# Row sums of reciprocals: the halves of a row paired, and one reciprocal for two elements

## The chip, the cores and the metric

The kernel runs on one core of a Trainium2 chip. The metric is the device time of one execution in microseconds (us); the times given are medians of several runs of the same program.

## The reference

```python
# x: (32, 512, 1024) float32, |N(0,1)| + 1e-6, all positive
def reference(x):
    return np.sum(1.0 / x, axis=-1).astype(np.float32)   # (32, 512)
```

There are 32 x 512 = 16384 rows of 1024 elements (67.1 MB), and each is reduced to one number, the sum of its reciprocals.

## The kernel before, in words

The 16384 rows are laid out as 128 partitions with 128 rows each; the view `x_v` (line 31) is `[p, f, d]`, so that one partition reads its rows from one contiguous stretch of memory. Each row is worked on whole, by one of two ways to a reciprocal, and then summed on VectorE. Nothing uses TensorE, and GpSimd (POOL) does nothing but set four constants.

The list `TILES` (line 23) cuts the 128 rows of a partition into groups `(ta, tv)`: 13 groups of (7, 1), smaller ones at the start and at the end. In a group:

- `tv` rows (17 in all) go to tile `xv` (line 66) by a DMA of their own (line 67), and VectorE takes their reciprocal in place (line 68).
- `ta` rows (111 in all) go to tile `xa` (line 69) by a second DMA (line 70). ScalarE makes the reciprocal of all of them with two passes over the flat tile, in place: Ln (line 72), then Exp with scale -1 (line 73), since exp(-ln x) = 1/x.
- Then VectorE sums every row of the group by `row_sum` (line 51; its instruction carries line 52): a custom operation that adds the first half of the row to the second, writes the 512 sums to `scratch`, and accumulates them into one column of `sums`. Each of these is followed on the engine by a short instruction that reads the accumulator out into that column.

At the end one DMA writes `sums` to the output (line 80). All DMAs are issued on SyncE's queue (SP), in the order of the loop. `apool` and `vpool` have five buffers each, and a load is issued only once its buffer has been freed by the last row sum that reads it. The order of the instructions on each engine isn't written out by hand: the framework's scheduler sets it when the kernel is built and may move an instruction past others of its engine; at run time every engine goes through its own in that fixed order and waits for what each needs.

Of the kernel before, what the change touches and what calls it, by code (L numbers as in the profile page):

```python
# [1 line left out]

# [5 lines left out]


@with_exitstack
def kernel(
    ctx: ExitStack,
    tc: tile.TileContext,
    x: bass.AP,
    out: bass.AP,
):
    nc = tc.nc
    P = 128
    D = 1024  # L20
    F = 128

    TILES = [(2, 0), (3, 1), (6, 1)] + [(7, 1)] * 13 + [(4, 1), (3, 1), (2, 0)]
    assert sum(a + v for a, v in TILES) == F
    assert sum(v for a, v in TILES) == 17

    Ln = mybir.ActivationFunctionType.Ln
    Exp = mybir.ActivationFunctionType.Exp
    HALF = slice(None, D // 2), slice(D // 2, None)

    x_v = x.flatten_outer_dims().rearrange("(p f) d -> p f d", p=P)
    out_v = out.flatten().rearrange("(p f) -> p f", p=P)

    act_sets = list(get_activation_tables(nc.m.arch).keys())
    nc.scalar.add_instruction(  # L35
        mybir.InstLoadActFuncSet(
            name=nc.get_next_instruction_name(),
            act_func_set_id=act_sets.index("natural_log_exp_and_others"),
            ins=[],
            outs=[],  # L40
        )
    )

    apool = ctx.enter_context(tc.tile_pool(name="apool", bufs=5))
    vpool = ctx.enter_context(tc.tile_pool(name="vpool", bufs=5))
    opool = ctx.enter_context(tc.tile_pool(name="opool", bufs=1))

    sums = opool.tile([P, F], mybir.dt.float32)
    scratch = opool.tile([P, D // 2], mybir.dt.float32)

    def row_sum(src, c):
        nc.vector.tensor_tensor_reduce(  # L52
            out=scratch,
            in0=src[:, HALF[0]],
            in1=src[:, HALF[1]],
            scale=1.0,
            scalar=0.0,
            op0=mybir.AluOpType.add,
            op1=mybir.AluOpType.add,
            accum_out=sums[:, c : c + 1],  # L60
        )

    c0 = 0
    for t, (ta, tv) in enumerate(TILES):
        if tv:
            xv = vpool.tile([P, tv, D], mybir.dt.float32, tag="xv")
            nc.sync.dma_start(out=xv, in_=x_v[:, c0 + ta : c0 + ta + tv, :])
            nc.vector.reciprocal(out=xv, in_=xv)  # L68
        xa = apool.tile([P, ta, D], mybir.dt.float32, tag="xa")
        nc.sync.dma_start(out=xa, in_=x_v[:, c0 : c0 + ta, :])  # L70
        flat = xa.rearrange("p t d -> p (t d)")
        nc.scalar.activation(out=flat, in_=flat, func=Ln)  # L72
        nc.scalar.activation(out=flat, in_=flat, func=Exp, scale=-1.0)  # L73
        for j in range(ta):
            row_sum(xa[:, j], c0 + j)
        for j in range(tv):
            row_sum(xv[:, j], c0 + ta + j)
        c0 += ta + tv

    nc.sync.dma_start(out=out_v, in_=sums)  # L80


# [1 line left out]
_INS = ['x']  # L84
_OUTS = [((32, 512), 'float32')]


# [23 lines left out]
```

## Time and profile before

| | |
|---|---|
| median of 3 runs | 214.5 us (214.32 to 214.5) |
| span of the profiled execution, first to last instruction | 212.4 us |
| median less span: what lies around the span | 2.1 us |
| VectorE (DVE) busy | 197.0 us, 93% of the span |
| ScalarE (ACT) busy | 196.5 us, 92% |
| GpSimd (POOL) busy | 0.2 us |
| read from HBM | 67.11 MB, mean 316 GB/s over the span |

The profile is of one execution, and its time beyond the span isn't given apart from the runs'; the 2.1 us are the median of the runs less that span. Busy time counts an engine's instructions that compute; the share of 16 DMA engines can read a little over 1 in a short window, where packets overlap. A line such as L72 is line 72 of the kernel.

### The profile page before, as it was taken

Reading aid. Unit: us, or ns where it says so; the run is one execution under the profiler, and the core shown is the slowest. Engines: PE = TensorE matmul, PEld = TensorE weight load, DVE = VectorE, ACT = ScalarE, POOL = GpSimd, SP = SyncE. Lnnn points to the kernel's source line nnn. Section 1 sums busy time; section 2 is a strip of 40 time slices with the busy share of each in tenths; the row PEclk is TensorE's granted clock in tenths of the full one; section 3 lists DMA queues with packets and bytes.
Section 4 is the critical chain, followed back from the end, with each engine's and each line's share of the span. In section 5 each row is a group of like instructions: output and inputs, shape, how many; then the busy total and the mean of one; then the engine's idle time right before and its main releaser. Section 6 shows DMA issues by size and latency. Waiting matters only on the chain. (4 is left out here: it accounts for less than half of the span.)

```text
span 212.4 us, 455 instructions
## 1 busy us (share of the span) xinstructions
DVE 197.0 (93%) x273; ACT 196.5 (92%) x39; POOL 0.2 (0%) x4
## 2 busy tenths in 40 slices
DVE  0799999999999999999999999999999999999994
ACT  2794999999999999999999999999999999999960
POOL 0000000000000000000000000000000000000000
DMA  6999999999999999999998987969590715000000
GB/s 241 424 470 420 432 444 432 417 390 464 402 433 443 433 444 432 412 432 417 408 441 351 444 346 304 432 239 428 200 435 37 316 79 197 0 0 0 0 0 12
DMA packets 5330, 67.19 MB, mean 316 GB/s; under 512 B 592, under 2 KB 720, under 8 KB 2896
## 3 DMA queue, kind: packets, MB, share of 16 engines
q1 hardware_dynamic: 5328, 67.18, 75.4%
q14 instruction: 2, 0.02, 0.0%
HBM read 67.11 MB, written 0.07 MB: 316 GB/s over the span
## 5 line engine op out<-in xcount | busy, mean ns | idle before, releaser
L68 DVE RECIPROCAL xv<-xv 128x1024 f32<-128x1024 f32 x17 | 111.3, 6547 | 6.8 <-DMA xv<-in_x_dram 6.8
L72 ACT ACTIVATE xa<-xa 128x7168 f32<-128x7168 f32 (+4 forms) x19 | 98.2, 5174 | 7.7 <-DMA xa<-in_x_dram 7.7
L73 ACT ACTIVATE xa<-xa 128x7168 f32<-128x7168 f32 (+4 forms) x19 | 98.5, 5187 | 0.5
L52 DVE CUSTOM_DVE_ANT_0 scratch<-xa 128x512 f32<-128x512 f32 x111 | 75.8, 682 | 5.4 <-ACT xa L73 2.1
L52 DVE CUSTOM_DVE_ANT_0 scratch<-xv 128x512 f32<-128x512 f32 x17 | 11.7, 688 | 0.6
L52 DVE DVE_READ_ACCUMULATOR2_ANT sums<- 128x1 f32 x128 | 10.5, 82 | 0.0
L35 ACT ACT_TABLE_LOAD x1 | 1.3, 1283 | 0.7 <-PEq L95 0.7
L95 POOL MEMSET const-bfloat16-1.0<- 128x1 bf16 x1 | 0.1, 101 | 0.0
L95 POOL MEMSET const-uint8-127<- 128x1 uint8 x1 | 0.1, 101 | 0.0
L95 POOL MEMSET const-float32-0.0<- 128x1 f32 x1 | 0.1, 98 | 0.2 <-issue 0.2
L95 POOL MEMSET const-float32-1.0<- 128x1 f32 x1 | 0.1, 98 | 0.0
## 6 DMA issues: line engine op xcount, KB each, us to landing
xa<-in_x_dram SPq DMA_DIRECT2D x13, 3584.0 KB, 21.3
xv<-in_x_dram SPq DMA_DIRECT2D x17, 512.0 KB, 9.7
xa<-in_x_dram SPq DMA_DIRECT2D x2, 1536.0 KB, 7.8
xa<-in_x_dram SPq DMA_DIRECT2D x1, 3072.0 KB, 16.3
xa<-in_x_dram SPq DMA_DIRECT2D x2, 1024.0 KB, 4.8
xa<-in_x_dram SPq DMA_DIRECT2D x1, 2048.0 KB, 7.9
out_dram<-sums SPq DMA_DIRECT2D x1, 64.0 KB, 1.6
```

The costliest lines, as they stand in the source:

```text
L35: nc.scalar.add_instruction(mybir.InstLoadActFuncSet(name=nc.get_next_instruction_name(), act_func_set_id=act_sets.index("natural_log_exp_ ...
L52: nc.vector.tensor_tensor_reduce(out=scratch, in0=src[:, HALF[0]], in1=src[:, HALF[1]], scale=1.0, scalar=0.0, op0=mybir.AluOpType.add, op ...
L68: nc.vector.reciprocal(out=xv, in_=xv)
L72: nc.scalar.activation(out=flat, in_=flat, func=Ln)
L73: nc.scalar.activation(out=flat, in_=flat, func=Exp, scale=-1.0)
L95: nc = _bacc.Bacc("TRN2", target_bir_lowering=False, num_devices=1)
```

## The change

The reciprocals of two elements are taken from one reciprocal of their product: 1/a + 1/b = (a + b)/(ab). A row's first half is a, its second half b.

- The 128 rows of a partition are cut into 19 groups (`GROUPS`): (2,0), (3,1), fourteen of (7,1), (4,1), (2,1), (1,1). A group is one tile `xt` and one DMA (110 rows are paired, 18 are whole). There are four `xt` buffers.
- Paired rows are worked on in chunks of up to four (33 chunks in all, 28 of them in the groups of (7,1): one of four rows, one of three). GpSimd multiplies the halves into tile `pr`. ScalarE takes Ln of `pr` in place, with a scale S = 2^17, then Exp with scale -1 into tile `rc`, which lies in PSUM (two buffers of four banks). VectorE then does for each row one multiply and sum over 1024 elements: the row, seen as 2 x 512, times `rc` broadcast twice, times S, written over the row and accumulated into a column of `sums`.
- A whole row is done by ScalarE alone: Ln in place, then Exp in place with the accumulator output into its column of `sums`.
- VectorE's reciprocal, the tile `scratch` and the separate loads of `xv` are gone.

```diff
-    TILES = [(2, 0), (3, 1), (6, 1)] + [(7, 1)] * 13 + [(4, 1), (3, 1), (2, 0)]
+    GROUPS = [(2, 0), (3, 1)] + [(7, 1)] * 14 + [(4, 1), (2, 1), (1, 1)]
+    CH = 4
+    S = float(2**17)
...
-    apool = ctx.enter_context(tc.tile_pool(name="apool", bufs=5))
-    vpool = ctx.enter_context(tc.tile_pool(name="vpool", bufs=5))
+    xpool = ctx.enter_context(tc.tile_pool(name="xpool", bufs=4))
+    ppool = ctx.enter_context(tc.tile_pool(name="ppool", bufs=4))
     opool = ctx.enter_context(tc.tile_pool(name="opool", bufs=1))
+    rpool = ctx.enter_context(
+        tc.tile_pool(name="rpool", bufs=2, space=bass.MemoryType.PSUM)
+    )
...
-    for t, (ta, tv) in enumerate(TILES):
-        if tv:
-            xv = vpool.tile([P, tv, D], mybir.dt.float32, tag="xv")
-            nc.sync.dma_start(out=xv, in_=x_v[:, c0 + ta : c0 + ta + tv, :])
-            nc.vector.reciprocal(out=xv, in_=xv)
-        xa = apool.tile([P, ta, D], mybir.dt.float32, tag="xa")
-        nc.sync.dma_start(out=xa, in_=x_v[:, c0 : c0 + ta, :])
-        flat = xa.rearrange("p t d -> p (t d)")
-        nc.scalar.activation(out=flat, in_=flat, func=Ln)
-        nc.scalar.activation(out=flat, in_=flat, func=Exp, scale=-1.0)
-        for j in range(ta):
-            row_sum(xa[:, j], c0 + j)
-        for j in range(tv):
-            row_sum(xv[:, j], c0 + ta + j)
-        c0 += ta + tv
+    for np_, ns in GROUPS:
+        n = np_ + ns
+        xt = xpool.tile([P, n, D], f32, tag="xt")
+        nc.sync.dma_start(out=xt, in_=x_v[:, c0 : c0 + n, :])
+        for s in range(0, np_, CH):
+            m = min(CH, np_ - s)
+            pr = ppool.tile([P, m, H], f32, tag="pr")
+            nc.gpsimd.tensor_tensor(
+                out=pr, in0=xt[:, s : s + m, :H], in1=xt[:, s : s + m, H:], op=mult
+            )
+            nc.scalar.activation(out=pr, in_=pr, func=Ln, scale=S)
+            rc = rpool.tile([P, m, H], f32, tag="rc")
+            nc.scalar.activation(out=rc, in_=pr, func=Exp, scale=-1.0)
+            for j in range(m):
+                row = xt[:, s + j, :].rearrange("p (h e) -> p h e", h=2)
+                nc.vector.tensor_tensor_reduce(
+                    out=row,
+                    in0=row,
+                    in1=rc[:, j, :].unsqueeze(1).to_broadcast([P, 2, H]),
+                    scale=S,
+                    scalar=0.0,
+                    op0=mult,
+                    op1=add,
+                    accum_out=sums[:, c0 + s + j : c0 + s + j + 1],
+                )
+        if ns:
+            nc.scalar.activation(out=xt[:, np_:n, :], in_=xt[:, np_:n, :], func=Ln)
+            for j in range(np_, n):
+                nc.scalar.activation(
+                    out=xt[:, j, :],
+                    in_=xt[:, j, :],
+                    func=Exp,
+                    scale=-1.0,
+                    accum_out=sums[:, c0 + j : c0 + j + 1],
+                )
+        c0 += n
```

## Rows read from the trace of the kernel before

**Rows 1.** The page: busy time, and the span in 40 slices.

```profile
DVE 197.0 (93%) x273; ACT 196.5 (92%) x39; POOL 0.2 (0%) x4
...
DMA  6999999999999999999998987969590715000000
```

**Rows 2.** Timeline, one period: start us, us, engine, line, tiles, shapes, idle before.

```profile
54.24 6.16 ACT L72 ACTIVATE xa<-xa 128x7168 f32<-128x7168 f32 x1
...
54.37 0.69 DVE L52 CUSTOM_DVE_ANT_0 scratch<-xa 128x512 f32<-128x512 f32 x1 [0.15 <-ACT xa L73]
...
55.10 0.69 DVE L52 CUSTOM_DVE_ANT_0 scratch<-xa 128x512 f32<-128x512 f32 x1
...
56.45 6.55 DVE L68 RECIPROCAL xv<-xv 128x1024 f32<-128x1024 f32 x1
60.44 6.18 ACT L73 ACTIVATE xa<-xa 128x7168 f32<-128x7168 f32 x1
...
66.52 6.16 ACT L72 ACTIVATE xa<-xa 128x7168 f32<-128x7168 f32 x1
```

**Rows 3.** SP's waits: who waited for whom, us in total, times, longest us.

```profile
SPq L67 <- DVE sums L52: 133.6, 12, 16.8
```

**Rows 4.** Windows by stage: engines' busy us, clock, DMA share, GB/s.

```profile
0.00:2.00 2.00, 0.00 (x0) 1.27 (x1) 0.20 (x4) 1.00 0.19 41
2.00:5.60 3.60, 0.00 (x0) 0.01 (x1) 0.00 (x0) 1.00 0.94 366
5.60:24.00 18.40, 16.94 (x15) 14.23 (x5) 0.00 (x0) 1.00 1.03 440
24.00:60.00 36.00, 34.99 (x40) 35.91 (x7) 0.00 (x0) 1.00 1.01 429
60.00:118.00 58.00, 56.20 (x86) 57.84 (x11) 0.00 (x0) 1.00 0.98 417
118.00:185.00 67.00, 65.20 (x86) 66.81 (x12) 0.00 (x0) 1.00 0.66 269
```

**Rows 5.** Groups of instructions, shapes apart: busy us, mean ns, idle before.

```profile
L68 DVE RECIPROCAL xv<-xv 128x1024 f32<-128x1024 f32 x17 | 111.3, 6547 | 6.8 <-DMA xv<-in_x_dram 6.8
...
L72 ACT ACTIVATE xa<-xa 128x7168 f32<-128x7168 f32 x13 | 80.1, 6160 | 0.0
L52 DVE CUSTOM_DVE_ANT_0 scratch<-xa 128x512 f32<-128x512 f32 x111 | 75.8, 682 | 5.4 <-ACT xa L73 2.1
L52 DVE CUSTOM_DVE_ANT_0 scratch<-xv 128x512 f32<-128x512 f32 x17 | 11.7, 688 | 0.6
L52 DVE DVE_READ_ACCUMULATOR2_ANT sums<- 128x1 f32 x128 | 10.5, 82 | 0.0
...
L72 ACT ACTIVATE xa<-xa 128x3072 f32<-128x3072 f32 x2 | 5.5, 2754 | 1.0 <-DMA xa<-in_x_dram 1.0
```

**Rows 6.** DMA issues of the page: count, KB each, us to landing.

```profile
xa<-in_x_dram SPq DMA_DIRECT2D x13, 3584.0 KB, 21.3
xv<-in_x_dram SPq DMA_DIRECT2D x17, 512.0 KB, 9.7
```

**Rows 7.** Timeline, the end: the last row sum and the output's DMA.

```profile
209.16 0.69 DVE L52 CUSTOM_DVE_ANT_0 scratch<-xa 128x512 f32<-128x512 f32 x1
209.78 0.08 DVE L52 DVE_READ_ACCUMULATOR2_ANT sums<- 128x1 f32 x1
209.89 0.34 SPq L80 DMA_DIRECT2D out_dram<-sums  x1
```

More of the change, by code (lines that the diff above doesn't have):

```diff
@@ L18 @@
     nc = tc.nc
+    f32 = mybir.dt.float32
     P = 128
     D = 1024
+    H = D // 2
     F = 128
-    TILES = [(2, 0), (3, 1), (6, 1)] + [(7, 1)] * 13 + [(4, 1), (3, 1), (2, 0)]
-    assert sum(a + v for a, v in TILES) == F
-    assert sum(v for a, v in TILES) == 17
+    CH = 4
+    S = float(2**17)
+    GROUPS = [(2, 0), (3, 1)] + [(7, 1)] * 14 + [(4, 1), (2, 1), (1, 1)]
+    assert sum(a + b for a, b in GROUPS) <= F
     Ln = mybir.ActivationFunctionType.Ln
     Exp = mybir.ActivationFunctionType.Exp
-    HALF = slice(None, D // 2), slice(D // 2, None)
+    mult = mybir.AluOpType.mult
+    add = mybir.AluOpType.add
     x_v = x.flatten_outer_dims().rearrange("(p f) d -> p f d", p=P)
@@ L42 @@
     )
-    apool = ctx.enter_context(tc.tile_pool(name="apool", bufs=5))
-    vpool = ctx.enter_context(tc.tile_pool(name="vpool", bufs=5))
+    xpool = ctx.enter_context(tc.tile_pool(name="xpool", bufs=4))
+    ppool = ctx.enter_context(tc.tile_pool(name="ppool", bufs=4))
     opool = ctx.enter_context(tc.tile_pool(name="opool", bufs=1))
[L48 to L61, printed above, removed]
@@ new lines @@
+    sums = opool.tile([P, F], f32)
+    c0 = 0
+    for np_, ns in GROUPS:
[34 more added lines that the diff above has]
+        c0 += n
@@ L80 @@
+    assert c0 == F, c0
     nc.sync.dma_start(out=out_v, in_=sums)
```

## The prediction

> **What bounds the kernel now.** I read the page first, then one period of the timeline, SP's waits and the windows by stage. The page shows VectorE and ScalarE both busy over 92% of the span, while the DMA line runs full for its first half and then thins out [rows 1]. In the timeline one group of eight rows takes 66.52 - 54.24 = 12.28 us on ScalarE, whose two passes follow each other without a gap, and VectorE waits 0.15 us a period for ScalarE [rows 2]. So both engines set the pace, at 12.28 us for eight rows (4.19 MB, 342 GB/s). The loads aren't the limit: SP stands 133.6 us waiting for row sums to free buffers [rows 3]. Left alone, the DMA runs faster: 440, 429 and 417 GB/s in three stretches at a share of 0.98 to 1.03, and 269 GB/s once the buffers are full [rows 4]. The question is how far the engines fall below the loads' own pace of 8 x 0.5243 MB / 429 GB/s = 9.78 us for eight rows, and what follows the last load.
>
> **ScalarE.** It now passes over half-length products of 110 rows and whole rows of 18. From the forms of 7168 and 3072 elements [rows 5]: (6160 - 2754) / 4096 = 0.8315 ns an element, and 2754 - 3072 x 0.8315 = 200 ns fixed. A pair of passes starts 12.28 us after the one before although it lasts 6.16 + 6.18 us [rows 2], so 0.06 is taken off a pair. A (7,1) group has 2 x (2048 + 1536 + 1024) = 9216 elements in six instructions: 7.66 + 1.20 - 0.18 = 8.68 us. The accumulator's read-out on ScalarE is in no row; VectorE's takes 82 ns [rows 5], so I add 0.08 (bounds 0 and 0.20, a whole fixed part): 8.76 us. Exp into PSUM isn't shown either: anything from a gain to a loss of one fixed part, 0.20 for each of two Exps; I take none, since the same stream with 0.4 more, 9.2, stays below 9.78. In all: 149504 elements x 0.8315 = 124 us, 102 instructions x 0.20 = 20, less 51 x 0.06, plus 1: 143 us where it was 196.5.
>
> **VectorE.** The 17 reciprocals go (111.3 us), and 128 sums over 512 pairs become 110 over 1024. A 512-element sum takes 0.69 us, and the next one starts 0.73 after it [rows 2, 5]. How the new one grows is in no row. At least by 512 elements at ScalarE's rate: 0.69 + 0.43 = 1.12. At most by a second 512 less the fixed part, which can't be much below the 0.08 of the one-element read-out: 0.69 + 0.61 = 1.30. I take the middle, 1.21, and 0.04 to the next start: 1.25 us a row, 8.75 us a group (8.1 to 9.4), 137 us in all. The operand in PSUM is unshown; the nearest rows are these two-input float32 sums, so I add nothing, and as the upper end 0.20 (a rival below).
>
> **GpSimd.** Its only rows here are constants, 0.2 us in all [rows 1]. A product of 512 pairs is nearest to VectorE's two-input 512-element sum, 0.69 us; the far end is half a reciprocal of 1024, 3.27 us [rows 5]. I take 0.69: 2.8 us for four rows, 4.8 us a group, 76 in all. It decides nothing until 9.78 / 7 = 1.40 us a row.
>
> The Trainium skill, "GPSIMD Engine Reference", section "Performance versus the Vector engine", speaks against this placing: an elementwise float32 operation of two inputs over 2048 elements is given 4497 ns there, about twice VectorE's time. By that estimate a chunk of four rows takes 4.5 us and a group 7.9, still under 9.78, and the sum below would be 178.1; no run here shows it.
>
> **Loads and waits.** Eight rows now come by one DMA instead of two. One of 3.5 MB takes 21.3 us from issue to landing, behind others in the queue [rows 6], so size isn't new; issues fall from 37 to 20 and stay hidden behind transfers. Five buffers of each kind become four. A buffer is held for its load (9.8), the first product (2.8), Ln and Exp of 2048 (3.7), seven rows on VectorE (8.75), and some 2.5 of issue and start: 27.6 us, against 4 x 9.78 = 39.1 at the loads' pace. So 11 us are spare and SP always has a further load queued. New are ScalarE's waits for GpSimd, with Exp and the whole row queued behind, and VectorE's for Exp; in the steady state each engine idles about 1 us a group, and nobody downstream is late, because the next data lands only after 9.78 us.
>
> **The sum.** The loads bound all but the ends. By 5.6 us, 2.0 x 41 + 3.6 x 366 GB/s = 1.40 MB have come [rows 4]; the other 65.71 MB at 429 take 153.2 us: last landing 158.8. (At 440, 154.9; at 417, 163.2.) The last (7,1) group lands ten rows, 12.2 us, earlier. ScalarE starts it 2.8 us later and ends it 8.8 after that, 0.6 before the last landing. Then, by the same prices, (4,1) takes 5.9, (2,1) 4.2 and (1,1) 3.3 us, all landed and multiplied by then: 12.7 after the last landing, 13.0 with two hand-offs of 0.15 [rows 2]. VectorE's last row ends before that, at 11.9. From the last sum, at 209.86, to the end of the span it took 2.5 us [rows 7]. Span: 158.8 + 13.0 + 2.5 = 174.3 us, against 212.4. Around the profiled span 2.1 us lie to the median of 214.5: **176.4 us**.
>
> **Rivals.**
>
> *ScalarE or VectorE still sets the pace.* If the PSUM operand costs VectorE 0.20 a row, a group takes 7 x 1.45 = 10.15 us; over fourteen groups that is 5 us more, about 182. It decides from 1.40 us a row. The same price comes from an order in which ScalarE stands before a whole row whose load is still under way: the scheduler does move work forward, as the reciprocal at 56.45 among older sums shows [rows 2]. One group too early fits into the 11 us spare; two hold a buffer for some 41 us, 0.4 a group over 39.1: again 182.
>
> *The read rate doesn't hold.* Rates fall from stretch to stretch [rows 4]; 417 throughout gives 163.2 + 15.5 + 2.1 = 181. At 342 GB/s, the pace of the kernel before, it would be 5.6 + 192.1 + 15.5 + 2.1 = 215, no gain at all; a fall far below 417 gets 0.01.
>
> A rule of the Trainium skill goes that way: "SBUF — State Buffer", section "Summary: rules for kernel authors", tells one to reckon transfers between HBM and SBUF at about 358 GB/s, and by that this kernel would take 207 us. The trace speaks against it: 429 GB/s over 36 us.
>
> *GpSimd is slow.* At x us a row the time is 5.6 (first landing) + 110 x + 3 (last passes) + 4.6 (the end): 13.2 + 110 x. It passes the loads from x = 1.48, is 214.5 at x = 1.83 and 373 at the far end.
>
> *GpSimd and VectorE shut each other out (slower).* Both work in SBUF at the same time, which nothing in this trace shows, since GpSimd did nothing [rows 1]. If a product can't run while a row sum does, the two add up: 0.69 + 1.25 = 1.94 a row, 13.2 + 110 x 1.94 = 227 us. It decides from a sum of 1.83. For it speaks that GpSimd has been left free of such work so far and no row excludes it; against it, that the new sum reads only one operand from SBUF.
>
> The Trainium skill bears on that: "SBUF — State Buffer", section "Who interferes with whom", has VectorE keep GpSimd's reads out only with two inputs in SBUF or in a two-port mode, and here the reciprocals are in PSUM; no run here shows it.
>
> *The change doesn't run as overlapped as written.* VectorE writes its products back over the tile whose later rows GpSimd still has to read. If the second product waited for the first four rows, a group would be a chain: 2.8 + 3.7 + 5.0 + 2.1 = 13.6 us, fourteen of them 190, with 19 before and 23 after: 232 us.
>
> **How the numbers follow.** Loads as the bound, 172 to 181 by their rate: 0.67, since three engines each come in under 9.78 us at their own rows' prices. ScalarE, VectorE or the order sets the pace (181 to 190): 0.14. GpSimd between 1.48 and 1.83: 0.04, beyond it 0.03. Loads far slower, but short of 215: 0.01. Shut out 0.07, chained 0.03, no visible change 0.01. Faster is 0.67 + 0.01 + 0.14 + 0.04 = 0.86, slower 0.13; the bound of 0.2%, 0.4 us, is about what a measurement of this kernel can tell from no change. The range is 171 to 195: below, 440 GB/s (-3.9) and a gain on PSUM; above, the engines' rivals and GpSimd up to 1.65. It leaves out some 0.16.
>
> **What would show it.** Right: a DMA line at 9 until about 159 us, a read-out's DMA some 15 us later; ScalarE and VectorE at about 140 us of busy time, idling before products and Exp. Wrong: gaps in the DMA line before 150 us; a product over 1.4 us a row, or longer when a row sum runs beside it; row sums over 1.4 us; VectorE or ScalarE without idle time in the middle.

## The result, and the profile after

The changed kernel takes 180.19 us (four runs, 180.13 to 180.47) against 214.44 for the kernel before, measured again beside it: a ratio of 0.8406, 95% interval 0.8394 to 0.8417. Forecast were 176.4 us, faster, and a range of 171 to 195. The span of the profiled execution is 178.0 us, with 2.1 to 2.2 around it as before; the sum had 174.3.

From the page of the changed kernel, engines and the DMA line, to be laid beside [rows 1]:

```profile
DVE 127.0 (71%) x220; ACT 141.5 (79%) x121; POOL 125.2 (70%) x37
DMA  6999999999998999999999999999999999851000
```

VectorE and ScalarE were at 93 and 92% and are now at 71 and 79%. No engine is the bound by its share; the DMA line is the one that stays at 9, for 32 of 40 slices. The windows by stage say it in GB/s (columns as in [rows 4]):

```profile
5.60:24.00 18.40, 5.88 (x10) 9.43 (x10) 9.59 (x3) 1.00 1.00 430
24.00:60.00 36.00, 24.23 (x42) 30.24 (x24) 28.80 (x9) 1.00 1.01 437
60.00:118.00 58.00, 48.47 (x84) 50.57 (x43) 46.80 (x13) 1.00 1.01 433
118.00:185.00 67.00, 48.39 (x84) 49.95 (x45) 39.72 (x11) 1.00 0.60 253
```

The groups of instructions with shapes apart (columns as in [rows 5]) have the new prices:

```profile
L81 DVE CUSTOM_DVE_ANT_1 xt<-xt,rc 128x1024 f32<-128x1024 f32 x110 | 126.9, 1217 | 48.5 <-issue 38.3 <-ACT rc L78 10.2
L73 POOL TENSOR_TENSOR pr<-xt 128x2048 f32<-128x2048 f32 x15 | 67.9, 4528 | 31.0 <-DMA xt<-in_x_dram 31.0
L73 POOL TENSOR_TENSOR pr<-xt 128x1536 f32<-128x1536 f32 x15 | 51.8, 3452 | 2.5 <-DMA xt<-in_x_dram 2.5
L76 ACT ACTIVATE pr<-pr 128x2048 f32<-128x2048 f32 x15 | 28.5, 1897 | 3.0 <-POOL pr L73 2.9
L78 ACT ACTIVATE rc<-pr 128x2048 f32<-128x2048 f32 x15 | 28.0, 1864 | 0.0
...
L94 ACT ACTIVATION_READ_ACCUMULATOR xt<-xt 128x1 f32 x18 | 3.4, 186 | 0.0
```

A row sum over 1024 elements costs 1217 ns, a product of four rows 4528 ns, and GpSimd's idle time stands in front of the first product of a group, until a load lands. Who waits for whom, in us, times, and the longest:

```profile
POOL pr L73 <- DMA xt<-in_x_dram: 38.6, 16, 6.3
ACT pr L76 <- POOL pr L73: 27.0, 18, 5.9
```

The first engine of the chain waits for data, the second for the first. SP waits for freed buffers about as long as before [rows 3], 147.7 us in 15 waits, but now other loads are under way meanwhile: the DMA share stays at 1.00 to 1.01 until 118 us. GpSimd's timeline shows the pace (two products of a group in one line, x2), and where it ends:

```profile
88.78 7.95 POOL L73 TENSOR_TENSOR pr<-xt 128x2048 f32<-128x2048 f32 x2 [1.77 <-DMA xt<-in_x_dram]
98.49 7.94 POOL L73 TENSOR_TENSOR pr<-xt 128x2048 f32<-128x2048 f32 x2 [1.77 <-DMA xt<-in_x_dram]
...
148.03 15.98 POOL L73 TENSOR_TENSOR pr<-xt 128x2048 f32<-128x2048 f32 x5 [2.75 <-DMA xt<-in_x_dram]
```

98.49 - 88.78 = 9.71 us a group, and every group begins when a load lands. The last (7,1) group landed at 148.03. From there the end is told by ScalarE's and VectorE's timelines:

```profile
152.59 1.91 ACT L76 ACTIVATE pr<-pr 128x2048 f32<-128x2048 f32 x1 [0.50 <-POOL pr L73]
156.01 1.48 ACT L76 ACTIVATE pr<-pr 128x1536 f32<-128x1536 f32 x1 [1.50 <-POOL pr L73]
157.40 3.23 ACT L78 ACTIVATE rc<-pr 128x2048 f32<-128x2048 f32 x2
...
159.38 1.22 DVE L81 CUSTOM_DVE_ANT_1 xt<-xt,rc 128x1024 f32<-128x1024 f32 x1 [2.62 <-issue]
...
174.23 1.22 DVE L81 CUSTOM_DVE_ANT_1 xt<-xt,rc 128x1024 f32<-128x1024 f32 x1
...
175.48 0.35 SPq L104 DMA_DIRECT2D out_dram<-sums  x1
```

The instruction at 156.01 is the second chunk's Ln. It stands on ScalarE in front of the first chunk's Exp (157.40), although the program text has them the other way, and it waits 1.50 us for the second product. So VectorE, which had nothing to do for 2.62 us (the profile names no releaser there; Exp's end is the one that fits), gets its first reciprocals at 159.3. Then it sums 14 rows without a gap, 1.142 us apart, to 175.4.

### The profile page after: what moved, and what is told of

It is laid out like the page before. It is cut to its first block, busy times and chain, and to the rows that moved or that the text cites. A ratio compares the mean times of both kernels' runs of the same rounds, so it can differ in the third digit from the quotient of the medians.

```text
span 178.0 us, 550 instructions
## 1 busy us (share of the span) xinstructions
DVE 127.0 (71%) x220; ACT 141.5 (79%) x121; POOL 125.2 (70%) x37
## 5 line engine op out<-in xcount | busy, mean ns | idle before, releaser
L81 DVE CUSTOM_DVE_ANT_1 xt<-xt,rc 128x1024 f32<-128x1024 f32 x110 | 126.9, 1217 | 48.5 <-issue 38.3
L73 POOL TENSOR_TENSOR pr<-xt 128x1536 f32<-128x1536 f32 (+3 forms) x33 | 125.0, 3808 | 38.6 <-DMA xt<-in_x_dram 38.6
L76 ACT ACTIVATE pr<-pr 128x1536 f32<-128x1536 f32 (+3 forms) x33 | 53.4, 1618 | 27.1 <-POOL pr L73 27.0
L78 ACT ACTIVATE rc<-pr 128x1536 f32<-128x1536 f32 (+3 forms) x33 | 51.2, 1579 | 0.1
L92 ACT ACTIVATE xt<-xt 128x1024 f32<-128x1024 f32 x18 | 18.8, 1042 | 3.6 <-DMA xt<-in_x_dram 3.6
L94 ACT ACTIVATE xt<-xt 128x1024 f32<-128x1024 f32 x18 | 19.0, 1056 | 0.5
L81 DVE DVE_READ_ACCUMULATOR2_ANT sums<- 128x1 f32 x110 | 9.1, 83 | 0.0
L94 ACT ACTIVATION_READ_ACCUMULATOR xt<-xt 128x1 f32 x18 | 3.4, 186 | 0.0
```

The lines of the kernel that those rows point to most:

```text
L73: nc.gpsimd.tensor_tensor(out=pr, in0=xt[:, s : s + m, :H], in1=xt[:, s : s + m, H:], op=mult)
L76: nc.scalar.activation(out=pr, in_=pr, func=Ln, scale=S)
L78: nc.scalar.activation(out=rc, in_=pr, func=Exp, scale=-1.0)
L81: nc.vector.tensor_tensor_reduce(out=row, in0=row, in1=rc[:, j, :].unsqueeze(1).to_broadcast([P, 2, H]), scale=S, scalar=0.0, op0=mult, op ...
L92: nc.scalar.activation(out=xt[:, np_:n, :], in_=xt[:, np_:n, :], func=Ln)
L94: nc.scalar.activation(out=xt[:, j, :], in_=xt[:, j, :], func=Exp, scale=-1.0, accum_out=sums[:, c0 + j : c0 + j + 1],)
```

## The experiments

The first four ask what the loads, the order, PSUM and the number of buffers are worth.

**e1: ScalarE in the order of the program text.**

Every pass of ScalarE goes through `act`, which adds an edge of order, without a wait, behind the pass before it.

```diff
+    def act(**kw):
+        i = nc.scalar.activation(**kw)
+        i = getattr(i, "ins", i)
+        if last[0] is not None:
+            tc.add_manual_dep(
...
+        last[0] = i
...
-            nc.scalar.activation(out=pr, in_=pr, func=Ln, scale=S)
+            act(out=pr, in_=pr, func=Ln, scale=S)
```

> ScalarE's instructions are kept in the order of the program text, so that each Exp stands right behind its Ln; nothing else changes. Theory (the order on ScalarE is part of the last stretch): Exp of the last (7,1) group's first chunk no longer waits for the second product, so it starts some 2.9 us earlier, the 1.5 us gap on ScalarE there closes, and the end moves by about 2.0 us: 178.2 us, with the steady period unchanged at 9.71 us. Rival (the loads bound everything, an order on an engine with spare time costs nothing): 180.2 us.

179.69 us, 0.5 less: the expectation was 1.5 too hopeful. ScalarE's end in e1's timeline:

```profile
154.85 1.88 ACT L68 ACTIVATE rc<-pr 128x2048 f32<-128x2048 f32 x1
...
172.36 0.60 ACT L68 ACTIVATE rc<-pr 128x512 f32<-128x512 f32 x1
172.89 2.13 ACT L68 ACTIVATE xt<-xt 128x1024 f32<-128x1024 f32 x2
```

Exp does start at 154.85 instead of 157.40. But now ScalarE ends last: the text's order leaves a whole row (2.13 us and its read-out) behind the last Exp, where the scheduler had put it in front. It is also dearer throughout: a group, gap taken off, takes 8.87 us (83.97 to 93.70 less 0.86), where the changed kernel's order takes 8.59 (84.02 to 93.73 less 1.12). Another order does it in 8.33 (e3b).

**e2: the reciprocals in SBUF.**

```diff
-        tc.tile_pool(name="rpool", bufs=2, space=bass.MemoryType.PSUM)
+        tc.tile_pool(name="rpool", bufs=2)
```

> The tile rc lies in SBUF instead of PSUM, so that VectorE's row sum reads two inputs from SBUF while GpSimd multiplies. Theory A (the two engines shut each other out as soon as VectorE reads twice from SBUF): 1.14 + 1.13 = 2.27 us a row, and 13.2 + 110 x 2.27 = 263 us, with either products or row sums drawn out or waiting. Theory B (they share without loss wherever the operand lies): 180 us, with products at 4.53 and row sums at 1.22 us or less.

260.72 us, ratio 1.2153 (1.2135 to 1.2171) to the kernel before: slower than that, and near the 263 of theory A. Groups of instructions of e2, then a stretch of its timeline:

```profile
L81 DVE CUSTOM_DVE_ANT_1 xt<-xt,rc 128x1024 f32<-128x1024 f32 x110 | 236.8, 2220 | 19.0 <-ACT rc L78 10.2 <-issue 8.8
...
L73 POOL TENSOR_TENSOR pr<-xt 128x1536 f32<-128x1536 f32 x15 | 63.0, 4199 | 19.0 <-ACT rc L78 16.5 <-DMA xt<-in_x_dram 2.5
```

```profile
100.92 1.21 DVE L81 CUSTOM_DVE_ANT_1 xt<-xt,rc 128x1024 f32<-128x1024 f32 x1
...
101.43 9.45 POOL L73 TENSOR_TENSOR pr<-xt 128x2048 f32<-128x2048 f32 x2 [7.25 <-ACT rc L78]
...
102.07 5.53 DVE L81 CUSTOM_DVE_ANT_1 xt<-xt,rc 128x1024 f32<-128x1024 f32 x1
...
107.53 4.42 DVE L81 CUSTOM_DVE_ANT_1 xt<-xt,rc 128x1024 f32<-128x1024 f32 x1
...
111.89 1.21 DVE L81 CUSTOM_DVE_ANT_1 xt<-xt,rc 128x1024 f32<-128x1024 f32 x1
112.06 1.91 ACT L78 ACTIVATE rc<-pr 128x2048 f32<-128x2048 f32 x1 [5.33 <-DVE sums L81]
```

A row sum takes 1.21 us while GpSimd is idle. One that runs into a product lasts 5.53 or 4.42 us, a product and its own time together. The two engines don't share time, they take turns: 110 x 1.142 + 125 us of products = 251 of the 258.5 us of span. The edit also moves Exp's output into SBUF, but that isn't the cause: the row sum at 111.89 runs beside an Exp that writes there and still takes 1.21 us. The rival of the prediction, on its slower side, is thus real; it applies when both operands of the row sum lie in SBUF, and the place of one small tile keeps it away.

**e3 and e3b: fewer loads.**

```diff
-        nc.sync.dma_start(out=xt, in_=x_v[:, c0 : c0 + n, :])
+        if g < 6 or n < 8:
+            nc.sync.dma_start(out=xt, in_=x_v[:, c0 : c0 + n, :])
+        else:
+            nc.sync.dma_start(out=xt[:, 4:, :], in_=x_v[:, c0 + 4 : c0 + n, :])
```

> From the fifth (7,1) group on only four of the eight rows of a group are loaded (ten groups, 40 of 128 rows fewer, 48.6 us of loading); the other rows are what the buffer holds from four groups earlier, so these sums are of other data. All work on the engines stays. Theory (the loads set the pace of 9.71 us, and ScalarE with 8.65 us is next): ten groups shorter by 1.06, some 170 us, ScalarE without gaps. Rival 1 (some chain of waits sets the pace and the loads merely follow): 180 us. Rival 2 (nothing else is near the loads): 180 less nearly 48, about 135 to 140 us.

> As e3_half_loads (four of eight rows loaded from the fifth (7,1) group on, the other sums of older data), but each small group has a buffer of its own, so that no load at the end waits for one; pr has three buffers. Theory (loads set the pace of 9.71 us, ScalarE at the 8.34 us seen in e3 is next): ten groups shorter by 1.37 us, 166.5 us. Rival (the 173 of e3 is a pace of its own and not the late small loads): 173 us.

In both, the loads that are left out leave older data in the buffers, so their sums are not the kernel's result, only their time counts. e3 took 173.27 us, between its theories. Its groups did speed up, to 8.34 us, but the (7,1) groups had been given fixed buffers and the small ones only two to share, and GpSimd waited up to 20 us for a small load. With that mended, e3b took 166.58 us, as expected. ScalarE's timeline in e3b, the first Ln of three groups in turn, without a gap between its passes:

```profile
103.87 1.89 ACT L83 ACTIVATE pr<-pr 128x2048 f32<-128x2048 f32 x1
...
112.20 1.89 ACT L83 ACTIVATE pr<-pr 128x2048 f32<-128x2048 f32 x1
...
120.53 1.90 ACT L83 ACTIVATE pr<-pr 128x2048 f32<-128x2048 f32 x1
```

So the loads set the 9.71 us, and the next limit, ScalarE at 8.33, lies only 14% below it (11% by the 8.59 of the changed kernel's own order).

**e4: five buffers.**

```diff
-    xpool = ctx.enter_context(tc.tile_pool(name="xpool", bufs=4))
+    xpool = ctx.enter_context(tc.tile_pool(name="xpool", bufs=5))
```

> xpool has five buffers instead of four. In the changed kernel the last three loads are issued 9.7 to 10.1 us apart, each as a buffer comes free, and the DMA line thins out from 152 us. Theory (those loads are late without anybody waiting, since GpSimd works without a gap from 148.0 us to the end of its products): last landing some 3.5 us earlier, time unless the last (7,1) group lands earlier too the same, 179.2 to 180.2 us (the last (7,1) group came 1.0 us later than the cadence). Rival (the starved loads are what the end waits for): 176.5 us.

180.39 us (180.28 to 180.85), no change. Windows at the end, of the changed kernel, then of e4:

```profile
152.00:156.00 4.00, 4.00 (x9) 2.00 (x3) 4.00 (x3) 1.00 0.80 340
156.00:160.00 4.00, 1.38 (x3) 3.99 (x3) 4.00 (x1) 1.00 0.54 184
160.00:164.00 4.00, 4.00 (x9) 3.97 (x5) 4.00 (x3) 1.00 0.20 84
```

```profile
152.00:156.00 4.00, 4.00 (x9) 2.29 (x3) 4.00 (x2) 1.00 0.98 416
156.00:160.00 4.00, 1.36 (x3) 3.68 (x3) 4.00 (x2) 1.00 0.52 216
160.00:164.00 4.00, 4.00 (x7) 3.97 (x5) 4.00 (x3) 1.00 0.00 0
```

The last loads do come earlier (nothing moves after 160 us), but GpSimd (third busy column) is at 4.00 of 4 us in both: nobody waited for them.

**e5: the products on VectorE.**

```diff
-            nc.gpsimd.tensor_tensor(
+            nc.vector.tensor_tensor(
```

> The products go from GpSimd to VectorE (the same operation on the same tiles); GpSimd does nothing. Theory (VectorE's two-input products cost what its two-input sums of before did, 0.6 to 0.7 us for 512 pairs, and nothing excludes them as GpSimd is idle): a (7,1) group takes VectorE 8.0 + 7 x 0.58 = 12.0 us instead of 8.0 and sets the pace: 180.2 + 14 x (12.0 - 9.7) = 212 us, about the kernel before. Rival (two inputs from SBUF are slow for VectorE in themselves, as a row sum of 2.2 us in e2 could be read): products of 4 us and more for four rows, over 240 us.

214.14 us, ratio 0.9985 (0.9975 to 0.9996): the whole gain gone. From its groups of instructions:

```profile
L73 DVE TENSOR_TENSOR pr<-xt 128x2048 f32<-128x2048 f32 x15 | 34.3, 2287 | 1.1 <-DMA xt<-in_x_dram 1.1
```

The same product of four rows costs VectorE 2.29 us and GpSimd 4.53, and yet the slower engine is the right place, since it has the time. The row also shows that two operands in SBUF are no burden to VectorE alone: 1.12 ns an element, no more than the row sum with one operand in PSUM (1217 ns for 1024).

**e6: one product of two issued twice.**

```diff
+            if m == 3:
+                nc.gpsimd.tensor_tensor(
+                    out=pr, in0=xt[:, s : s + m, :H], in1=xt[:, s : s + m, H:], op=mult
+                )
```

> Each product of three rows is issued twice on GpSimd, so that a (7,1) group costs GpSimd 7.95 + 3.4 = 11.35 us, 1.62 us a row; nothing else changes. Theory (GpSimd decides from 1.40 us a row, and then sets the pace): first product at 20.1, fourteen groups of 11.35, the small groups' 8.1 (their product of three included), then passes and a row sum of some 3.5, 2.5 and 2.1 us: 195 us; the prediction's 13.2 + 110 x gives 192. Rival (GpSimd's spare time takes it): 180 us.

202.11 us. GpSimd's timeline:

```profile
100.38 7.95 POOL L73 TENSOR_TENSOR pr<-xt 128x2048 f32<-128x2048 f32 x2
108.41 3.44 POOL L77 TENSOR_TENSOR pr<-xt 128x1536 f32<-128x1536 f32 x1
111.80 7.95 POOL L73 TENSOR_TENSOR pr<-xt 128x2048 f32<-128x2048 f32 x2
...
180.35 8.09 POOL L73 TENSOR_TENSOR pr<-xt 128x2048 f32<-128x2048 f32 x3
```

ScalarE's, its end:

```profile
196.01 0.19 ACT L98 ACTIVATION_READ_ACCUMULATOR xt<-xt 128x1 f32 x1
```

111.80 - 100.38 = 11.42 us a group, 1.63 a row, with no wait for loads, as expected: at that price GpSimd sets the pace. Of the 7 us missing, 1.3 lie in the products: the last ended at 188.4, where 187.1 had been reckoned (20.1 + 14 x 11.35 + 8.1). The other 6 lie behind them: 3.5 us were allowed for passes and a row sum, and ScalarE still had passes up to 196.2, whole rows among them.

**e8 and e9: the last group alone.** In group 15, the last (7,1), an edge of order keeps a chunk's Ln behind the Exp of the chunk before; e9 has the `ch` line besides.

```diff
+            if prev is not None:
+                tc.add_manual_dep(
+                    getattr(ln, "ins", ln),
+                    prev.name,
...
+            prev = getattr(ex, "ins", ex) if g == 15 else None
...
+        ch = 2 if g == 15 else CH
```

> Only in the last (7,1) group is the second chunk's Ln kept behind the first chunk's Exp; ScalarE's order is else that of the changed kernel, but for the last Exp with read-out, which now stands last. Theory (e1 gained only 0.5 us because the plain order costs ScalarE overlap everywhere and leaves a whole row behind the last Exp, not because the wait for the second product is free): the 1.5 us gap of ScalarE at 154.5 closes, row sums start 2.9 us earlier, and the end is then ScalarE's work from 152.6 on without a gap, some 172.2 instead of 175.5: 177.2 us. Rival (the order isn't what the end waits for): 179.7 to 180.2 us.

> As e8, and the last (7,1) group's products are made in chunks of two rows, so that its first product takes 2.35 us instead of 4.53. Theory (ScalarE is at the group before until 152.1 us, so a product that ends at 150.4 instead of 152.5 brings its first Ln forward by 0.5 us at most, and two more pairs of passes cost some 0.4): as e8 within 0.5 us, about 177.2 us. Rival (the price of the first product stands in the end's sum in full, as the prediction had it): 2.2 us less than e8, 175 us.

e8 took 178.32 us, 1.9 less than the changed kernel; e9 180.19, no better than that. e8's end:

```profile
154.70 1.88 ACT L88 ACTIVATE rc<-pr 128x2048 f32<-128x2048 f32 x1
...
156.86 1.22 DVE L92 CUSTOM_DVE_ANT_1 xt<-xt,rc 128x1024 f32<-128x1024 f32 x1
...
165.46 1.22 DVE L92 CUSTOM_DVE_ANT_1 xt<-xt,rc 128x1024 f32<-128x1024 f32 x1 [0.53 <-issue]
...
173.63 0.35 SPq L115 DMA_DIRECT2D out_dram<-sums  x1
```

The reciprocals are there at 156.6, and VectorE takes them up at 156.86, when it is through with the group before: 2.5 us earlier than in the changed kernel (159.38), not 2.9. Before 165.46 it waits for ScalarE again, for the (4,1) group's Exp, which costs 0.6. That is why 1.9 came of the 2.9. In e9 the first product ended 2.2 us earlier, but four chunks meet two PSUM buffers, and Exp waits for row sums. From its waits, then the same place on VectorE's timeline:

```profile
ACT rc L89 <- DVE sums L93: 2.2, 3, 1.4
```

```profile
167.09 1.22 DVE L93 CUSTOM_DVE_ANT_1 xt<-xt,rc 128x1024 f32<-128x1024 f32 x1 [2.15 <-issue]
```

So ScalarE comes later to the (4,1) group, VectorE waits 2.15 us for it where it waited 0.53, and that undoes e8's gain. Both expectations of e9 missed this. It does show that an earlier first product brings nothing by itself: here too VectorE was busy with the group before until 156.86.

**e7: a version meant to be faster.** ScalarE's passes go through `act` as in e1; besides:

```diff
-    GROUPS = [(2, 0), (3, 1)] + [(7, 1)] * 14 + [(4, 1), (2, 1), (1, 1)]
+    GROUPS = (
+        [(2, 0), (3, 1)]
+        + [(4, 0), (3, 1)] * 13
+        + [(3, 0)] * 4
+        + [(2, 1)] * 2
+    )
...
-    xpool = ctx.enter_context(tc.tile_pool(name="xpool", bufs=4))
+    xpool = ctx.enter_context(tc.tile_pool(name="xpool", bufs=9))
```

> A version meant to be faster, against the last stretch: ScalarE in program order as in e1, groups of four rows, (4,0) and (3,1) in turn, thirteen of each, then four of (3,0) and two of (2,1) with nothing left behind them, nine buffers of four rows. Work: 111 paired rows, 17 whole. Theory (after the last landing at about 158 us only what is queued on the engines counts, and smaller groups queue less): last row sum at 166 to 168 instead of 175.5, 171 to 173 us. Rival (the last stretch is as long, since ScalarE pays a fixed part for more instructions and goes without a gap): 180 us.

174.47 us, ratio 0.8130 (0.8119 to 0.8141): 5.7 us below the changed kernel, but above the 171 to 173 expected. (It pairs 112 rows and leaves 16 whole, not 111 and 17.) From its windows, then VectorE's last row:

```profile
60.00:118.00 58.00, 47.42 (x83) 52.23 (x42) 47.18 (x12) 1.00 1.01 429
...
156.00:160.00 4.00, 4.00 (x7) 3.25 (x3) 3.76 (x2) 1.00 0.78 329
160.00:164.00 4.00, 4.00 (x9) 3.94 (x5) 2.71 (x2) 1.00 0.01 6
```

```profile
168.34 1.22 DVE L102 CUSTOM_DVE_ANT_1 xt<-xt,rc 128x1024 f32<-128x1024 f32 x1
```

The loads run at 429 GB/s in the middle and hardly any bytes come after about 160 us; the last row sum ends at 169.6 instead of 175.5. That fits its theory, that less stands in the engines' queues when the last load lands. But group size, buffers, order and the number of paired rows changed together here, and no run takes them apart. Some 10 us from the last bytes to the end of the sums are left.

## Why the prediction was right, and where its sizes were off

**The bound.** Right. The loads set the pace at 9.71 us a group where 9.78 was forecast; e3b, which does the same work on the engines with fewer loads, fell to ScalarE's pace and by about the 13.7 us that ten shorter groups give (180.2 - 166.6 = 13.6). That the two agree so closely is partly chance: ScalarE begins the last (7,1) group 15.4 us earlier there (137.20 for 152.59), and the end behind it is longer.

**ScalarE.** 141.5 us of busy time for a forecast of 143. The group's 8.76 us was 8.59 in the changed kernel, and 8.33 and 8.87 in two other orders (e3b, e1). The read-out is 0.19, not 0.08, but inside its bounds; Exp into PSUM takes 1864 ns where Ln of the same length into SBUF takes 1897.

**VectorE.** The middle of the bounds, 1.21 us, was 1.217 measured: luck, since no row chose between 1.12 and 1.30. The 0.04 to the next start was wrong in sign: rows start 1.142 us apart, so 8.0 us a group instead of 8.75. The PSUM operand costs nothing: 1.217 us against 1.21 in e2 where GpSimd was idle. The rival built on 0.20 for it falls.

**GpSimd.** The term that was mis-sized: 0.69 us a row was taken from VectorE's row, 1.13 was measured (4528 / 4), so 7.95 us a group and 125 in all, not 4.8 and 76. The Trainium skill's 4497 ns for 2048 elements ("GPSIMD Engine Reference", "Performance versus the Vector engine") agrees with 4528 within 1%, and the sum by it, 178.1, was nearer to 180.2 than mine. But not by the way it took, a later first product: in e9 that product ends 2.2 us earlier than in e8, and the row sums start no earlier. The forecast held in spite of this price because 1.13 still lies under 1.40 us a row, and that was the margin, not the pricing; e6, at 1.63, shows what lies above it.

**Loads and waits.** A further load was queued throughout, but not to the end: the last three were issued as buffers came free, and the DMA share fell to 0.80, 0.54 and 0.20. The step had counted four buffers of eight rows and forgotten that the last ones hold five, three and two. It cost nothing that can be told from e4's time.

**The sum.** Span 178.0 for 174.3, 3.7 us more, in two parts. The last (7,1) group landed at 148.03, not 146.6: 1.4. Its load came 1.0 us behind the cadence, and an earlier one 0.6. Missing buffers weren't the cause (with five, in e4, GpSimd waits 2.76 us there instead of 2.75); what was isn't shown. From there the sums ended at 175.46, 27.4 us later instead of 25.2: 2.2. Of these, e8 gives back 1.9 by an ordering edge in the last group, where the second chunk's Ln had stood ahead of the first chunk's Exp. The sum had let ScalarE go through the group without a gap and come last, 1.1 us behind VectorE. In truth VectorE's 14 rows behind the first Exp of that group were the end, and that Exp stood behind a wait for GpSimd: the first row sum began 11.35 us after the landing, and by the sum's own prices it would have been some 6.7. Of these 4.7 us, 1.5 came back by luck, since 14 rows took 1.142 us each and not 1.25. That the scheduler moves work forward was in the text, but was priced for a load, not for a product.

**The rivals.** *ScalarE or VectorE sets the pace:* neither did, at 8.59 and 8.0 us a group for 9.71. The order that the rival feared, a whole row ahead of its load, cost 3.6 us in all and none in the middle. *Shut out:* the mechanism exists (e2, 260.7 us; the forecast's own formula with the measured prices gives 263), and didn't apply because one operand is in PSUM. With both engines at work side by side in the changed kernel, row sums stay at 1217 ns on the mean and the products at 4528. The Trainium skill's rule ("SBUF — State Buffer", "Who interferes with whom") says both halves of this: VectorE with two inputs in SBUF locks out a GpSimd instruction that reads there, with one it doesn't. Both halves are now in runs here, e2 and the changed kernel. *Read rate:* it held, 437 and 433 GB/s in the middle; the 358 of the same page's "Summary: rules for kernel authors" lies below each of the three stretches from 5.6 to 118 us. *Chained:* the two products of a group run back to back (x2 in 7.95 us), so nothing waits for VectorE's writes into the same tile. *GpSimd slow:* its threshold lies between two runs, 1.13 us a row (loads set the pace) and 1.63 (GpSimd does, e6). Its formula gave 192 for e6's 202: some 4 us short in the products, and 6 because the 3 us for the last passes left out whole rows.

## What to carry to other kernels

When two engines share a chain, ask first which time the stage's transfers need, then give each engine any work that fits under it: a product that took twice as long on the idle engine was worth 34 us, as it was the busy one that had no room. Look at where each operand lies before putting two engines side by side, since one operand's place made 80 us here. And when the transfers are the bound, what is left to gain is the stretch behind the last one: small last groups, and the order in which the engines go through them.

## What had not been expected of the hardware

- The exclusion of e2 shows in the profile not as idle time, but as longer instructions: a row sum of 1.21 us becomes one of 5.53 us, and VectorE counts as 92% busy, of which close to half is waiting (236.8 us for 110 rows of 1.21). Products are stretched as well (4199 ns for 3452 on the mean).
- Passes of ScalarE that don't depend on each other follow closer: six passes and a read-out take 8.33 us interleaved, and 8.87 us when each Exp stands behind its own Ln (e3b, e1), 0.5 us a group. In e1 an Exp starts 0.04 us after its own Ln ends (85.88, 85.92), and the next Ln 0.07 us before that Exp ends (87.73, 87.80).
- GpSimd's product goes by 1272, 2347, 3452 and 4528 ns for 512, 1024, 1536 and 2048 elements: some 2.1 ns an element and 0.2 us fixed.
